# A trunk step of HGRN2, attention and convolution: four tiles instead of three grow during the first modulation, and the background modulation is paced differently

## The chip, the cores and the metric

The kernel runs on one core of a Trainium2 chip. The metric is the device time of one execution in microseconds (us), the median of several runs. PE is TensorE, DVE is VectorE, ACT is ScalarE, POOL is GpSimd and SP is SyncE, whose queue carries most loads.

## What is computed

Two trunk layers work on 640 tokens (128 of context, 512 latent) with 2048 channels. Cut to what matters here:

```python
def trunk_layer(x, shift, scale, gate, w_in_l, w_out_l, ...):
    h = x * (1 + scale) + shift
    z = h @ w_in_l
    aq, ak, av, ag, hq, hi, hff, hfb, hgate, ca, cb, cgate = jnp.split(z, SPLIT_POINTS, axis=-1)
    ...
    mix = jnp.concatenate([att * silu(ag), hg_out * silu(hgate), cv_out * silu(cgate)], axis=-1)
    out = mix @ w_out_l
    x_new = layer_norm(ALPHA * x + gate * out, ln_w_l, ln_b_l)
```

Shift, scale and gate of each layer are `silu(cond) @ ada_w_l + ada_b_l`, the modulation. The three branches are an HGRN2 gated recurrence in both directions (4 heads), windowed attention (8 heads) and a convolution over 31 positions with a layer norm.

## The kernel before

**The projections.** Tokens lie along the free dimension. The input projection of a layer is 52 tiles of 128 output channels by 640 tokens (list `NTILES`): tiles 0 to 15 are `hff, hfb, hi, hq` of the four HGRN heads, 16 to 19 the HGRN gates, 20 to 31 attention, 32 to 39 the convolution (`cb`, `ca` of four channel blocks), 40 to 51 gates. A float32 product is made of three products of rounded parts (`HH` and `HL` of the activations, `wh` and `wl` of the weights), so a tile takes 16 k-rows x 3 products x 2 pieces (256 and 384 columns, L1173 and L1175) = 96 matmuls. A tile accumulates in PSUM: `zt[0]` and `zt[1]` hold 1024 columns each, two banks (columns 0 to 511 and 512 to 1023), and `mb[0]` to `mb[3]` are one bank each. A tile in `zt` uses columns 256 to 511 and 512 to 895. Weights come in pieces of 256 KB, `raw` by SP's queue; ACT rounds them (L290, L286), and the low part comes by a second load that POOL issues (L292) or by a subtraction on DVE (L287).

**Stage 1.** The first layer's shift and scale are needed before anything else: `ada_pe` streams 64 tiles `adaw` of 512 KB through SP's queue, multiplies each on PE (four matmuls at L317), and for each of 8 steps `n` and 2 parts sums the result (two transposes at L327). After a step, two k-rows of `h` are built, and `start_mm(n - 1)` grows `NS` = 3 projection tiles by the two k-rows of the step before (12 matmuls a tile). The last block, `start_mm(7)`, runs after the last step. The fourth tile (tile 3, `hq` of head 0) is the first of the main loop.

**The main loop.** Each tile is 8 pieces of 12 matmuls, and after each piece `pump(3, rate)` lets up to three steps of the waiting generators emit their instructions: evacuations (`e_hf` takes a sigmoid and a logarithm of `hff` and `hfb` and scans them, `e_hi` copies, `e_hq` takes a Silu), the HGRN heads (`hg_main`), attention, convolution (`e_ca`, L1027 per tap) and its layer norm (`conv_ln`). The program thus fixes the order on each engine.

**HGRN.** A head works at levels 64, 32, 16, 8 and finer: POOL subtracts (L521, L524), ACT takes exponentials, DVE multiplies (L533, L534; L606, L607 at a finer level), PE multiplies in blocks of 32 (L540, in `compact`).

**Background modulation.** The other modulations, (layer, part) = (0,2), (1,1), (1,0) in layer 0 and (1,2) in layer 1, run on DVE: `ada_dve` loads 64 tiles `adawD` each and makes 256 products each at L362; a step is two products. Their pace is a credit: each pump adds `rate` to it and each whole unit buys a step.

```python
            rate = RATE[l][0 if i < 20 else 1 if i < 32 else 2 if i < 45 else 3]
```

In the output projection, which works in groups of columns, `pump(1, RWO ...)` does the same. By the program's order a main-loop tile has 4 to 10 such steps.

**The convolution's layer norm.** `total` adds four channel blocks (L1047, L1048), `split` parts the sum (L286, L287), PE sums over channels with ones (L426, L427), and L1068 subtracts the mean. ACT's squares (L1072) follow, and behind them, in ACT's order, an evacuation (L1096) and roundings of weights (L290, L291), from which POOL's L292 loads are issued.

## Time and profile before

| | |
|---|---|
| runs | 2252.66, 2254.46, 2255.24 us; median 2254.46 |
| profiled execution | 2252.99 us, its span 2251.1 us, so 1.9 us lie around the span |
| mean granted clock of PE | 0.992 |
| busy share of PE | 97% |
| HBM read | 383.46 MB |

The profile shows one execution. "Busy" is time in which the engine ran an instruction; "idle before, releaser" is time in which the engine stood and what ended it. A timeline row is the start in us, the duration, engine, line, operation, tile written and tiles read; in brackets the idle time before it and the instruction that ended it. A window row gives the busy time of every engine in a stretch.

### The profile page before, as it was taken

The numbers are of one execution on the slowest core, as the hardware profiler recorded it, in microseconds if no ns is written. First come the engines' busy times: TensorE is split into PE (matmuls) and PEld (weight loads), VectorE is DVE, ScalarE is ACT, GpSimd is POOL, SyncE is SP. The second block draws the span as 40 slices with busy tenths as digits, with TensorE's granted clock in tenths as the row PEclk, the third lists the DMA queues.
The fourth block names the chain that finished last, engine by engine and source line by source line (L and its number), as shares of the span: only waits on it lengthen the run. The fifth ranks groups of instructions, "written<-read, shape, count | busy, mean of one in ns | idle before, by whom it ended". The sixth has DMA issues, their size and how long they took to land.

```text
span 2251.1 us, 42122 instructions
## 1 busy us (share of the span) xinstructions
PE 2178.7 (97%) x15854; PEld 2077.2 (92%) x15854; DVE 1472.3 (65%) x3795; ACT 1142.6 (51%) x2047; POOL 616.0 (27%) x704
## 2 busy tenths in 40 slices
PE   6899999999999999999989999999999999999995
PEld 3699999999999999988989999999999999998895
DVE  2488889557669998676673666534655877234458
ACT  1177877546565335511165878764556543551111
POOL 0034334332222243300032344433222133330005
PEclk9999999999999999999999999999999999999998
DMA  9978787887777789964435777788776577685332
GB/s 371 400 191 203 184 200 188 206 218 182 170 159 170 190 193 229 272 197 135 118 130 135 160 173 163 158 193 186 162 153 129 114 170 157 144 196 178 96 97 103
DMA packets 210716, 403.60 MB, mean 179 GB/s; under 512 B 24816, under 2 KB 30672, under 8 KB 209872
## 3 DMA queue, kind: packets, MB, share of 16 engines
q1 hardware_dynamic: 138992, 271.85, 38.3%
q0 software_dynamic: 61600, 116.96, 30.3%
q10 hardware_dynamic: 9920, 12.10, 1.7%
q8 instruction: 124, 2.03, 0.4%
q14 instruction: 80, 0.66, 0.1%
HBM read 383.46 MB, written 12.11 MB: 176 GB/s over the span
## 4 chain that ended last, share of the span: by engine, by line
PE 77%; DVE 11%; DMA 4%; issue 3%; ACT 3%; POOL 1%; ACTq 0%; SPq 0%; DVEq 0%; POOLq 0%
PE z L1175 31%; PE z L1173 21%; PE z L1432 9%; PE m L1432 8%; DVE junk L362 4%; DMA x<-adaw 2%; PE m L948 2%; PE m L862 2%; PE m L916 1%; DMA s<-xT 1%; PE m L664 1%; DVE y1y L1414 1%; ACT s L1392 1%; DVE s L534 1%; DVE y1y L1415 0%
## 5 line engine op out<-in xcount | busy, mean ns | idle before, releaser
L1175 PE MATMUL z<-HH,wh 128*128 128x384 f32 x3296 | 1045.8, 338 | 0.0
L1173 PE MATMUL z<-HH,wh 128*128 128x256 f32 x3296 | 926.4, 283 | 1.6 <-DVE wh L287 0.9
L292 POOL DMA_DIRECT2D wh<-win x388 | 344.4, 933 | 1090.8 <-ACT wh L291 1021.5
L1173 PEld LDWEIGHTS z<-HH,wh 128*128 128x128 f32 x3296 | 619.4, 189 | 5.5 <-DVE wh L287 1.6
L1175 PEld LDWEIGHTS z<-HH,wh 128*128 128x128 f32 x3296 | 620.0, 188 | 1.5
L1175 PE MATMUL z<-HL,wh 128*128 128x384 f32 x1648 | 557.6, 338 | 0.0
L362 DVE SCALAR_TENSOR_TENSOR junk<-raw,s 128x256 bf16<-128x256 f32 x1024 | 503.8, 492 | 52.1 <-DMA raw<-adawD 24.4
L1173 PE MATMUL z<-HL,wh 128*128 128x256 f32 x1648 | 461.3, 280 | 0.0
L1173 PEld LDWEIGHTS z<-HL,wh 128*128 128x128 f32 x1648 | 311.0, 189 | 0.0
L1175 PEld LDWEIGHTS z<-HL,wh 128*128 128x128 f32 x1648 | 309.9, 188 | 0.0
L291 ACT ACTIVATE wh<-wh 128x512 fp32r<-128x512 f32 x400 | 253.1, 633 | 79.4 <-PE z L1175 68.4
L290 ACT CAST wh<-raw 128x512 fp32r<-128x512 f32 x400 | 244.0, 610 | 71.2 <-issue 36.2
L286 ACT CAST wh<-raw 128x512 fp32r<-128x512 f32 x136 | 83.0, 621 | 305.0 <-PE m L1432 156.6
L1027 DVE SCALAR_TENSOR_TENSOR s<-s,sm,s 128x655 f32<-128x655 f32 x240 | 231.2, 963 | 6.3
L1432 PE MATMUL z<-wh,HH 128*128 128x512 f32 (+1 forms) x640 | 182.0, 368 | 0.0
L1432 PE MATMUL m<-wh,HH 128*128 128x512 f32 (+1 forms) x640 | 173.8, 357 | 0.0
L287 DVE TENSOR_TENSOR wh<-raw,wh 128x512 fp32r<-128x512 f32 x138 | 92.6, 687 | 122.9 <-ACT wh L286 120.2
L1432 PEld LDWEIGHTS z<-wh,HH 128*128 128x128 f32 x640 | 116.1, 189 | 20.0
L1432 PEld LDWEIGHTS m<-wh,HH 128*128 128x128 f32 x640 | 114.1, 189 | 17.5
L1432 PE MATMUL z<-wh,HL 128*128 128x512 f32 (+1 forms) x320 | 117.7, 368 | 0.0
L1432 PE MATMUL m<-wh,HL 128*128 128x512 f32 (+1 forms) x320 | 114.3, 357 | 0.0
L1096 ACT ACTIVATE s<-z 128x640 f32<-128x640 f32 x32 | 22.5, 703 | 151.6 <-PE z L1175 142.8
(555 smaller groups left out, 2745.2 us busy)
## 6 DMA issues: line engine op xcount, KB each, us to landing
raw<-win SPq DMA_DIRECT2D x416, 256.0 KB, 4.2
wh<-win POOLq DMA_DIRECT2D x388, 256.0 KB, 5.5
raw<-adawD SPq DMA_DIRECT2D x256, 256.0 KB, 4.0
x<-adaw SPq DMA_DIRECT2D x64, 512.0 KB, 8.3
raw<-wout SPq DMA_DIRECT2D x128, 256.0 KB, 2.8
s<-crow SPq DMA_DIRECT2D x32, 256.0 KB, 5.9
s<-xT ACTq DMA_DIRECT2D x16, 320.0 KB, 7.1
s<-s ACTq DMA_DIRECT2D x80, 64.0 KB, 3.8
```

What stands on the lines that cost most here:

```text
L286: act.copy(hi, src)
L287: (lo_eng or dve).tensor_tensor(lo, src, hi.bitcast(F32), op=ALU.subtract)
L290: act.copy(hi, r)
L291: act.activation(lo, hi.bitcast(F32), AF.Copy, scale=-1.0)
L292: pool.dma_start(out=lo, in_=w.bitcast(F32R), accum_op=ALU.add)
L362: dve.scalar_tensor_tensor(junk, r[:, 256 * n:256 * n + 256], 1.0, rows[0][:, 256 * c:256 * c + 256], op0=ALU.mult, op1=ALU.mult, accum_ou ...
L862: pe.matmul(b[:, 0:w], lhsT=a_, rhs=k_, start=(n_ == 0), stop=(n_ == 2))
L948: pe.matmul(o, lhsT=v_, rhs=p_, start=(y == 0 and n_ == 0), stop=(y == len(bl) - 1 and n_ == 2))
L1027: dve.scalar_tensor_tensor(acc, u[:, t:t + AW], sm[:, cw + t:cw + t + 1], acc, op0=ALU.mult, op1=ALU.add)
L1173: pe.matmul(za, lhsT=w_, rhs=h_[:, 0:2, k, :], start=st_, stop=sp_)
L1175: pe.matmul(zb, lhsT=w_, rhs=h_[:, 2:5, k, :], start=st_, stop=sp_)
L1432: pe.matmul(bs[tt][:, 0:w], lhsT=h_[:, tt, k, :], rhs=w_[:, o:o + w], start=(k == 0 and n_ == 0), stop=(k == KT - 1 and n_ == 2))
```

## The change

`NS` becomes 4, so all four tiles of head 0 grow in stage 1. A class `Z` describes a tile by its two pieces. Tiles 0 and 1 stay in `zt[0]` and `zt[1]`. Tile 2 takes the free columns 0 to 255 of `zt[1]` and bank `mb[2]`; tile 3 those of `zt[0]` and `mb[3]`. Tile 0 and tile 3 so share bank 0 of `zt[0]`, and tiles 1 and 2 share bank 0 of `zt[1]`. Two matmuls of zeros open these banks, and the pieces in them neither start nor stop an accumulation. A `zt` is given back when both its tiles are evacuated, so the first tile of the main loop, now tile 4, takes `mb[0]` and `mb[1]`. Evacuations of the four take two instructions. The pace of layer 0's background modulation goes from (1.0, 0.85, 0.5, 1.2) to (0.6, 1.0, 0.6, 1.3), and in the output projection from 4/3 to 2.0.

```diff
--- before.py
+++ after.py
@@ -45,7 +45,7 @@
 W0 = 4
 WN = (0, 3, 4)
 CY = 5
-RWO = 4 / 3
+RWO = 2.0
 ODMA = 6
 WKEEP = 3
 FL = 3
@@ -71,7 +71,7 @@
 SMW = _o
 
 ADAD = [(0, 2), (1, 1), (1, 0), (1, 2)]
-RATE = ((1.0, 0.85, 0.5, 1.2), (0.5, 0.5, 0.0, 0.8))
+RATE = ((0.6, 1.0, 0.6, 1.3), (0.5, 0.5, 0.0, 0.8))
 BLOCK = object()
 
 
@@ -221,11 +221,22 @@
     pool.dma_start(out=crow.rearrange("a c k -> (a c) k"), in_=crs[0:16, 0:256])
     S.put(crs)
 
+    class Z:
+
+
+        def __init__(self, a, b, put, opens=True, closes=True):
+            self.a, self.b, self.put, self.opens, self.closes = a, b, put, opens, closes
+
     def zput(z):
-        if isinstance(z, tuple):
-            M.put(*z)
+        if isinstance(z, Z):
+            z.put()
         else:
             ZP.put(z)
+
+    def zparts(z):
+        if isinstance(z, Z):
+            return (slice(0, 256), z.a), (slice(256, T), z.b)
+        return ((slice(0, T), z[:, 256:896]),)
 
     def load_consts():
         sync.dma_start(out=cos, in_=A["cos"])
@@ -450,7 +461,8 @@
         st = hgset[l, j]
         Kt, GG, _, _ = hv(l, st)
         kd = Kt[:, T * d:T * d + T]
-        act.activation(kd, zsb(z), AF.Sigmoid, scale=-1.0)
+        for x, v_ in zparts(z):
+            act.activation(kd[:, x], v_, AF.Sigmoid, scale=-1.0)
         zput(z)
         yield
         s = yield from S.get()
@@ -483,11 +495,8 @@
         yield from wait(("hgset", l, j))
         v = hv(l, hgset[l, j])[3]
         s = yield from S.get()
-        if isinstance(z, tuple):
-            act.copy(s[:, 0:256], z[0][:, 256:512])
-            act.copy(s[:, 256:640], z[1][:, 0:384])
-        else:
-            act.copy(s[:, 0:T], zsb(z))
+        for x, v_ in zparts(z):
+            act.copy(s[:, x], v_)
         zput(z)
         yield
         yield
@@ -497,7 +506,8 @@
 
     def e_hq(l, j, z):
         yield from wait(("hgset", l, j))
-        act.activation(hv(l, hgset[l, j])[2], zsb(z), AF.Silu)
+        for x, v_ in zparts(z):
+            act.activation(hv(l, hgset[l, j])[2][:, x], v_, AF.Silu)
         zput(z)
         flags.add(("hq", l, j))
         yield
@@ -1160,7 +1170,8 @@
 
 
     def mm(l, i, z, ks, halves):
-        za, zb = (z[0][:, 256:512], z[1][:, 0:384]) if isinstance(z, tuple) else (z[:, 256:512], z[:, 512:896])
+        za, zb = (z.a, z.b) if isinstance(z, Z) else (z[:, 256:512], z[:, 512:896])
+        opens, closes = (z.opens, z.closes) if isinstance(z, Z) else (True, True)
         za = za.rearrange("p (a b) -> p a b", b=P)
         zb = zb.rearrange("p (a b) -> p a b", b=P)
         for k in ks:
@@ -1170,13 +1181,29 @@
             for n_, (w_, h_) in enumerate(((wh, HH), (wh, HL), (wl, HH))):
                 st_, sp_ = (k == 0 and n_ == 0), (k == KT - 1 and n_ == 2)
                 if 0 in halves:
-                    pe.matmul(za, lhsT=w_, rhs=h_[:, 0:2, k, :], start=st_, stop=sp_)
+                    pe.matmul(za, lhsT=w_, rhs=h_[:, 0:2, k, :], start=st_ and opens,
+                              stop=sp_ and closes)
                 if 1 in halves:
                     pe.matmul(zb, lhsT=w_, rhs=h_[:, 2:5, k, :], start=st_, stop=sp_)
 
 
-    NS = 3
-    zs = [zt[0], zt[1], (mb[2], mb[3])]
+    NS = 4
+    share = [2, 2]
+
+    def zs_put(n, *ms):
+        def put():
+            M.put(*ms)
+            share[n] -= 1
+            if not share[n]:
+                ZP.put(zt[n])
+        return put
+
+    zs = [Z(zt[0][:, 256:512], zt[0][:, 512:896], zs_put(0), False, False),
+          Z(zt[1][:, 256:512], zt[1][:, 512:896], zs_put(1), False, False),
+          Z(zt[1][:, 0:256], mb[2][:, 0:384], zs_put(1, mb[2]), False),
+          Z(zt[0][:, 0:256], mb[3][:, 0:384], zs_put(0, mb[3]), False)]
+    for z in zt:
+        pe.matmul(z[:, 0:512], lhsT=zd[0][:, 0:128], rhs=zd[0][:, 0:512], start=True, stop=False)
     M.f = deque(mb[0:2])
     ZP.f.clear()
     for k in range(6):
@@ -1252,8 +1279,12 @@
         for i in range(first):
             enqueue(i, zs[i] if l == 0 else zt[i])
         for i in range(first, NN):
-            pump_until(lambda: ZP.f)
-            z = ZP.f.popleft()
+            if l == 0 and i == first:
+                m0, m1 = M.f.popleft(), M.f.popleft()
+                z = Z(m0[:, 256:512], m1[:, 0:384], lambda: M.put(m0, m1))
+            else:
+                pump_until(lambda: ZP.f)
+                z = ZP.f.popleft()
             if i == HOLD0:
                 hold.add(0)
             rate = RATE[l][0 if i < 20 else 1 if i < 32 else 2 if i < 45 else 3]
```

Three places show what moves. First ACT at the end of stage 1. The names are `h00kt` (the gates of head 0), `z_99` and `z_100` (the tiles `zt[0]`, `zt[1]`), `m_` (a bank `mb`), `s_` (scratch). Before:

```order
L453 ACT_TABLE_LOAD
L453 ACTIVATE h00kt<-z_99 128x640
L461 ACT_TABLE_LOAD
L461 ACTIVATE s_143<-s_143 128x640
L453 ACT_TABLE_LOAD
L453 ACTIVATE h00kt<-z_100 128x640
L487 COPY s_137<-m_103 128x256
L488 COPY s_137<-m_104 128x384
```

And in the changed kernel:

```order
L465 ACT_TABLE_LOAD
L465 ACTIVATE h00kt<-z_99 128x256
L465 ACTIVATE h00kt<-z_99 128x384
L465 ACTIVATE h00kt<-z_100 128x256
L465 ACTIVATE h00kt<-z_100 128x384
L499 COPY s_143<-z_100 128x256
L499 COPY s_143<-m_103 128x384
L301 CAST wh_430<-raw_254 128x512
L302 ACTIVATE wh_431<-wh_430 128x512
L473 ACT_TABLE_LOAD
```

The evacuations come in two pieces, the four sigmoids stand together, and the logarithms (L461, now L473) behind the copies of tile 2. The piece of tile 0 in `z_99`'s first bank stands behind the last matmul of tile 3 in that bank; before, it stood behind tile 0's own last matmul.

Second, DVE in head 1 of layer 0 between levels 32 and 8 (`h01kt`, `h01q`: that head's gates and queries; L362 is the background's product). Before:

```order
L533 TENSOR_TENSOR s_137<-s_137,h01kt 128x2x10x32
L534 SCALAR_TENSOR_TENSOR s_1973<-s_1973,h01q 128x640
L362 SCALAR_TENSOR_TENSOR junk,aacc<-raw_250,s_135 128x256 x2
L362 SCALAR_TENSOR_TENSOR junk,aacc<-raw_516,s_135 128x256 x4
L362 SCALAR_TENSOR_TENSOR junk,aacc<-raw_518,s_135 128x256 x2
L533 TENSOR_TENSOR s_143<-s_143,h01kt 128x2x20x16
L534 SCALAR_TENSOR_TENSOR s_117<-s_117,h01q 128x640
L362 SCALAR_TENSOR_TENSOR junk,aacc<-raw_518,s_135 128x256 x2
L533 TENSOR_TENSOR s_139<-s_139,h01kt 128x2x40x8
```

And now, where L533, L534 and L362 are L543, L544 and L373:

```order
L543 TENSOR_TENSOR s_197<-s_197,h01kt 128x2x10x32
L544 SCALAR_TENSOR_TENSOR s_143<-s_143,h01q 128x640
L373 SCALAR_TENSOR_TENSOR junk,aacc<-raw_258,s_141 128x256 x4
L543 TENSOR_TENSOR s_2004<-s_2004,h01kt 128x2x20x16
L544 SCALAR_TENSOR_TENSOR s_2005<-s_2005,h01q 128x640
L373 SCALAR_TENSOR_TENSOR junk,aacc<-raw_168,s_141 128x256 x2
L543 TENSOR_TENSOR s_135<-s_135,h01kt 128x2x40x8
```

Between levels 32 and 16 stood 8 products and now 4; heads 2 and 3 have 6 there, and before every head of the layer had 8. From the level-8 product to the first one at L607 there were 8 in head 1, and now 4. In layer 1 nothing moves.

Third, DVE at the convolution's layer norm of layer 0, from the last addition of the sum (L1048, now L1058) over the split (L287, now L298) to the first subtraction of the mean (L1068, now L1078). Before:

```order
L1048 TENSOR_TENSOR s_143<-s_143,s_7282 128x640
L362 SCALAR_TENSOR_TENSOR junk,aacc<-raw_246,s_2825 128x256 x4
L362 SCALAR_TENSOR_TENSOR junk,aacc<-raw_166,s_3508 128x256 x4
L362 SCALAR_TENSOR_TENSOR junk,aacc<-raw_248,s_3508 128x256 x4
L287 TENSOR_TENSOR s_8607<-s_143,s_8606 128x640
L362 SCALAR_TENSOR_TENSOR junk,aacc<-raw_162,s_3508 128x256 x4
L362 SCALAR_TENSOR_TENSOR junk,aacc<-raw_246,s_3508 128x256 x4
L1068 SCALAR_TENSOR_TENSOR a00k<-m_102,s_6780 128x128
```

And now:

```order
L1058 TENSOR_TENSOR s_139<-s_139,s_6419 128x640
L373 SCALAR_TENSOR_TENSOR junk,aacc<-raw_164,s_145 128x256 x2
L373 SCALAR_TENSOR_TENSOR junk,aacc<-raw_168,s_145 128x256 x4
L373 SCALAR_TENSOR_TENSOR junk,aacc<-raw_260,s_2005 128x256 x4
L373 SCALAR_TENSOR_TENSOR junk,aacc<-raw_258,s_2005 128x256 x4
L298 TENSOR_TENSOR s_8523<-s_139,s_8522 128x640
L373 SCALAR_TENSOR_TENSOR junk,aacc<-raw_164,s_2005 128x256 x4
L373 SCALAR_TENSOR_TENSOR junk,aacc<-raw_168,s_2005 128x256 x4
L373 SCALAR_TENSOR_TENSOR junk,aacc<-raw_256,s_2005 128x256 x4
L373 SCALAR_TENSOR_TENSOR junk,aacc<-raw_258,s_2005 128x256 x2
L1078 SCALAR_TENSOR_TENSOR a00k<-m_104,s_5851 128x128
```

There were 12 products ahead of the split and 8 behind it, and now there are 14 and 14. Over the convolution as a whole, the background products from the first attention step after the tile `ca` 0 to the split go up by 22 (11 pairs). By the same order, from tile 20 to the split there are 48 more than before. Every group of the output projection but the last has 24 in place of 16. No product is added or removed in all.

## Rows read from the trace of the kernel before

**Rows 1.** Page, parts 1 and 5 of the whole run: busy time by engine; one costly group.

```profile
PE 2178.7 (97%) x15854; PEld 2077.2 (92%) x15854; DVE 1472.3 (65%) x3795; ACT 1142.6 (51%) x2047; POOL 616.0 (27%) x704
...
L362 DVE SCALAR_TENSOR_TENSOR junk<-raw,s 128x256 bf16<-128x256 f32 x1024 | 503.8, 492 | 52.1 <-DMA raw<-adawD 24.4
```

**Rows 2.** Waits of PE, whole run: us in total, times, longest us.

```profile
PE m L317 <- DMA x<-adaw: 19.1, 15, 6.7
PE m L327 <- DVE s L323: 11.9, 16, 3.6
```

**Rows 3.** Windows: length, then busy PE, PEld, DVE, ACT, POOL, PEclk, DMA share, GB/s.

```profile
90.60:103.30 12.70, 11.61 (x105) 9.25 (x104) 4.69 (x12) 1.46 (x2) 0.00 (x0) 0.85 1.02 408
103.30:114.30 11.00, 9.90 (x105) 7.55 (x105) 6.50 (x15) 3.02 (x5) 0.00 (x0) 1.00 1.04 400
114.30:125.00 10.70, 10.70 (x75) 10.70 (x75) 6.95 (x15) 7.47 (x10) 0.00 (x0) 1.00 0.60 200
125.00:139.60 14.60, 14.60 (x102) 14.58 (x101) 11.75 (x28) 11.28 (x18) 6.11 (x6) 1.00 0.72 174
```

**Rows 4.** Timeline of ACT and of DVE, first evacuation.

```profile
121.03 1.28 ACT L453 ACT_TABLE_LOAD   x1
122.32 0.70 ACT L453 ACTIVATE h00kt<-z 128x640 f32<-128x640 f32 x1
...
127.26 1.49 DVE L465 TENSOR_TENSOR_SCAN h00gg<-scanm,s 128x640 f32<-128x640 bf16 x1
```

**Rows 5.** Waits of PE, HGRN of layer 0 (125 to 420), then of layer 1.

```profile
PE m L540 <- DVE s L534: 5.0, 4, 1.4
PE m L540 <- DVE s L607: 3.1, 4, 1.3
...
PE m L540 <- DVE s L607: 1.1, 1, 1.1
```

**Rows 6.** Timelines of DVE and PE, head 1 of layer 0; idle before in brackets.

```profile
221.17 6.16 DVE L362 SCALAR_TENSOR_TENSOR junk<-raw,s 128x256 bf16<-128x256 f32 x1
...
228.66 0.82 DVE L533 TENSOR_TENSOR s<-s,h01kt 128x640 f32<-128x640 f32 x1
...
231.69 0.82 DVE L534 SCALAR_TENSOR_TENSOR s<-s,h01q 128x640 f32<-128x640 f32 x1
...
232.56 0.56 PE L540 MATMUL m<-s,s 128*32 128x32 f32 x40 [1.36 <-DVE s L534]
```

**Rows 7.** Timeline of POOL, the same stretch.

```profile
221.59 1.58 POOL L521 TENSOR_TENSOR s<-h01gg 128x640 f32<-128x640 f32 x1
```

**Rows 8.** Windows (columns as above), then timeline of DVE, convolution of layer 0.

```profile
640.00:660.00 20.00, 20.00 (x144) 19.87 (x144) 9.74 (x41) 13.26 (x29) 4.53 (x8) 1.00 0.72 165
...
780.00:800.00 20.00, 20.00 (x138) 20.00 (x137) 19.44 (x38) 5.65 (x10) 5.21 (x6) 1.00 0.87 201
...
757.45 0.29 DVE L1015 TENSOR_TENSOR s<-z,s 128x128 f32<-128x128 f32 x1 [1.36 <-PE z L1175]
...
758.26 0.90 DVE L1027 SCALAR_TENSOR_TENSOR s<-s,sm,s 128x655 f32<-128x655 f32 x1
...
759.88 2.77 DVE L1027 SCALAR_TENSOR_TENSOR s<-s,sm,s 128x655 f32<-128x655 f32 x3
```

**Rows 9.** Timelines of DVE and PE, convolution's layer norm, layer 0.

```profile
851.59 0.82 DVE L287 TENSOR_TENSOR s<-s,s 128x640 fp32r<-128x640 f32 x1
...
855.92 0.34 PE L427 MATMUL m<-s,ones 128*128 128x384 f32 x1
```

**Rows 10.** POOL's timeline, its line from 860 to 866, PE's timeline.

```profile
863.55 0.88 POOL L292 DMA_DIRECT2D wh<-win  x1 [1.50 <-ACT wh L291]
...
DMA to landing us min/median/max: 4.3/4.9/5.5
...
870.99 0.28 PE L1173 MATMUL z<-HH,wh 128*128 128x256 f32 x1
```

**Rows 11.** Timeline of DVE, start of layer 0's output projection.

```profile
957.03 0.42 DVE L362 SCALAR_TENSOR_TENSOR junk<-raw,s 128x256 bf16<-128x256 f32 x1 [10.04 <-DMA raw<-adawD]
```

## The prediction

> **What bounds the kernel now.** I read the page first: PE is busy for 97% of the span and DVE for 65% [rows 1]. So time can come only from PE's waits, or from where PE works at a lower clock, and the question for each edit is which wait it removes or makes. The list of PE's waits comes next. Two of them belong to stage 1: 19.1 us for the modulation's tiles and 11.9 us for DVE's sums of them [rows 2]. The windows then cut stage 1 into its steps: in 90.6 to 103.3 the DMA engines are full (share 1.02) and PE's mean granted clock is 0.85, so part of that step ran at the lower of its two levels; in 103.3 to 114.3 PE is busy for 9.90 of 11.00 us; from 114.3 on it never waits [rows 3]. In layer 0's HGRN part, PE waits eight times for DVE's multiplications, 5.0 + 3.1 = 8.1 us, and once, 1.1 us, in layer 1 [rows 5]. In the convolution PE waits for nothing, but DVE is busy for 19.44 of 20 us [rows 8]: that is where a little more work shows.
>
> The sum is made against the profiled execution, 2252.99 us (span 2251.1); the median of the runs shown is 1.5 us above it. About 0.2%, 4.5 us, is what a measurement of this kernel tells from no change.
>
> **Stage 1: gain 6.5 us.** The last two blocks of three tiles, 72 matmuls, take 10.70 us [rows 3], so a tile's 96 take 14.3 and its share of one block (12 matmuls) 1.78. Before, tile 3 ran alone in 125.0 to 139.6 [rows 3]. Now its eight blocks lie in stage 1. Two of them stand in the last two blocks, where PE never waits: 3.6. One stands in the step that PE bounds already: 1.8. The other five, 8.9 us, lie in steps in which PE waits for tiles, 19.1 us in all [rows 2]: nothing, except that 1 MB of weights more goes through the same full DMA engines. At the windows' 400 GB/s that is 2.6 us; I take 1.9, since step 90.6 to 103.3 was held partly by PE at the lower clock (bounds 1.3 and 2.6). Stage 1 thus ends 1.9 + 1.8 + 3.6 = 7.3 us later, at 132.2, with 14.3 us of tile 3 done: 7.0 gained. A fall of the clock like that in the window with 0.85 costs 0.15 x 12.7 = 1.9; I take off 0.5 for its chance. Bounds: 14.3 - 8.0 - 1.9 = 4.4, and 14.3 - 6.7 = 7.6. The two opening matmuls stand at the program's start, before the first tile has landed; if that cover were gone they would cost two matmuls of 512 columns, under 1 us by the 0.34 of one with 384 [rows 9].
>
> **The change of stages: loss 1.5 us.** ACT began on tile 0 at 121.0, inside the last block [rows 4]. Now tile 0's first piece shares a bank with tile 3, and the order shows its sigmoid behind tile 3's last matmul in that bank, so ACT begins at 132.2. Up to head 0's exponentials it then makes four table loads of 1.28 and some 16 passes of about 0.70 [rows 4], 16.3 us, to 148.5; a multiplication pair of 0.82 each, begun before the last exponential, ends by about 149.8. PE comes to head 0's products 1 1/8 tiles after the stage, at 132.2 + 16.1 = 148.3. So PE waits about 1.5 (0, if the scans and roundings overlap as they did; 3, if POOL holds DVE once as it did at 221.17 [rows 6]). The rest of the order does not move on PE: heads 1 to 3 stand where they stood. What no row of the kernel before shows is a bank shared by two tiles. The Trainium skill, PSUM — Partial Sum Buffer, section "PSUM bank collisions raise a hardware error", says that two engines may not touch one bank in the same partitions at once, at different columns either, and that the hardware does not stall but errs. That speaks against this change: it is why the wait can't be dropped. Were tile 0 evacuated as early as before, this term would be 0 and the sum 1.5 lower; no run yet shows it.
>
> **HGRN of layer 0: gain 6.8 us.** In head 1 an L362 takes 6.16 us, because POOL subtracts beside it from 221.59 on [rows 6, 7]. Three more products follow, then level 16 is multiplied from 228.66, and PE's wait for level 8 is 1.36 at 232.56 [rows 6]. With 4 products in place of 8, those that remain are over before POOL begins; level 16 can begin when POOL lets go at about 227.3, 1.3 earlier, and the wait goes or leaves 0.1. Ahead of L607 four products of 0.49 [rows 1] fewer give 2.0 against waits of 1.3 at most [rows 5]. Layer 1, with 4 products per gap, has a single wait of 1.1 [rows 5]. So of 8.1 us I take 6.8, leaving one wait as long as layer 1's or a little more; bounds 5 and 8.1. What is late next is nothing: PE's own products follow.
>
> **Attention: nothing.** Just ahead of the convolution, in 640 to 660, DVE is busy for 9.74 of 20 us [rows 8], which covers two products more a tile; with that cover gone they would be late as in the convolution.
>
> **The convolution of layer 0: loss 4.7 us.** In the stretch before the layer norm 22 products are added, 11 pairs. A pair between two taps costs 1.62 - 0.92 = 0.69 us (758.26 to 759.88, against a third of 2.77) [rows 8], so 7.6. DVE's one wait for PE there, 1.4 us, takes up some, and half of the 0.56 us in each of some five windows, another 1.4 [rows 8]: DVE is 4.8 late at the split. The split ended at 852.4 and PE needed it at 855.92 [rows 9], 3.5 later: PE waits 1.3. Behind the split stand 14 products of 0.49, so the subtraction of the mean begins at 852.4 + 4.8 + 6.9 = 864.1, in place of 856.3 (right behind PE's 855.92 + 0.34), 7.8 late. Queued behind it on ACT are squares, an evacuation and the roundings from which POOL issues loads: one was issued at 863.55, landed 4.3 later, and PE needed it at 870.99 [rows 10], 3.1 in hand. PE itself is 1.3 later, so it waits another 7.8 - 1.3 - 3.1 = 3.4. Bounds: 0, if DVE takes up all, and 4.1 + 3.4 = 7.5, if nothing.
>
> **Output projection of layer 0: nothing.** Each of three groups gets 8 products more, 3.9 us, in a stretch where DVE once waits 10.04 us for its tiles [rows 11]. Bounds 0 and 3.9.
>
> Sum: -6.5 + 1.5 - 6.8 + 4.7 = -7.1, so 2245.9 as the profiled execution counts, and **2247.4** as median. Its own range, from the likelier part of the bounds, is 2242 to 2253.
>
> **The rivals.**
>
> *DVE takes up the convolution's products.* For: the lateness is a difference of estimates. Against: 19.44 of 20. Time: -11.8, 2242.7.
>
> *Stage 1 gives nothing*, that is, the change doesn't do what it says: PE, which runs in order, is what ends each step, and the fourth tile only moves. For: 11.61 of 12.70 and 9.90 of 11.00 are busy. Against: 19.1 us of waits for tiles. Time: -6.8 + 1.5 + 4.7 = -0.6, 2253.9.
>
> *HGRN's waits stay*, because POOL and ACT set them and not the count of products. For: the multiplication can't begin before about 227.3 in any case, and every wait is short. Against: 3 products of those 8 lie behind that point. Time: -6.5 + 1.5 + 4.7 = -0.3, 2254.2. The Trainium skill, SBUF — State Buffer, section "Who interferes with whom", calls the ports that VectorE shares with GpSimd an exclusive lock. By that rule a multiplication with two inputs in SBUF is held as the product was, and this rival follows wherever POOL ends late; the trace agrees, with 6.16 for a product that takes 0.49 in the mean.
>
> *Slower: DVE never catches up from tile 20 on.* All 48 products that the order adds up to the split are late there: 48 x 0.49 = 23.5. The wait is then 23.5 - 3.5 = 20.0, and 3.4 behind it, so the sum is -11.8 + 23.4 = +11.6, 2266. It decides from a lateness of 16.4 us on (below 11.9 the change still gains). For: the convolution has no room, and its taps are one chain that waits in DVE's order. Against: from 640 to 660 DVE is idle for half the time [rows 8], which should take the attention's share, and it waits for PE once later, 1.4 us.
>
> **How the numbers follow.** The forecast 0.48, no loss in the convolution 0.20, no gain in stage 1 0.10, HGRN's waits stay 0.10, slower 0.12. The first has most of its own range (0.40) below 2249.9, which is faster by over 0.2%; with the second and a little of the next two that makes 0.62 faster, 0.24 the same and 0.14 slower. The range 2240 to 2255 holds the first two cases nearly whole and the next two by their centres; it leaves out the slower case and the ends.
>
> **What would show it.** Right: stage 1's last block ends near 132; PE's waits for L534 and L607 (now L544 and L617) fall from 8.1 to about 1; a wait of PE for the convolution's split and one for a weight piece some 15 us behind it, 4 to 5 us together. Wrong: a last block near 139 or a clock below 1.00 in it (stage 1); the L540 matmuls (now L550) waiting as before (HGRN); no wait at the split (first rival) or one above 12 us (slower).

## The result and the profile after

The changed kernel takes 2278.16 us (median of 5 runs, 2275.49 to 2281.34) against 2254.46 (5 runs of the kernel before): a ratio of 1.0105, 95% interval 1.0092 to 1.0119. It is 24 us slower, where 7 us faster was forecast. The profiled execution took 2281.34 us, the slowest of the five; its span is 2279.6, 28.5 more than before, so the parts below add up to more than the 24 us of the medians.

The first view is the busy time by engine, and the list of PE's waits (us in total, times, longest):

```profile
PE 2190.3 (96%) x15858; PEld 2084.8 (91%) x15858; DVE 1449.9 (64%) x3799; ACT 1136.8 (50%) x2045; POOL 613.8 (27%) x700
```

```profile
PE m L328 <- DMA x<-adaw: 13.1, 12, 6.9
PE m L338 <- DVE s L334: 12.5, 16, 4.2
PE m L438 <- DVE s L298: 6.8, 2, 5.0
...
PE m L550 <- DVE s L544: 5.7, 2, 4.5
PE m L583 <- DVE s L544: 3.6, 1, 3.6
PE m L872 <- DVE ats L887: 3.2, 1, 3.2
PE m L550 <- DVE s L617: 3.0, 3, 1.6
...
PE m L865 <- DVE wh L298: 2.4, 2, 2.3
PE z L1184 <- DMA wh<-win: 2.0, 3, 1.0
```

PE's busy share says almost nothing (97% before). The list does. L328 is the modulation's wait (L317 before) and fell from 19.1 to 13.1 [rows 2]: the fourth tile does fill waits of stage 1. Five waits that the kernel before did not have, or had shorter, matter below: L438 (the layer norm of the convolution), L583 and one L550 of 4.5 us (head 0), L872 and L865 (attention).

To see what each part lost, I take the start of a tile's first matmul in PE's timeline, before and after, and the growth of the difference from one to the next. The same is done for every experiment below (us, profiled executions; minus is faster than before; "end" is the span). The profiled executions lie up to 3.2 us from the medians that are given with the experiments, so a row shows where time goes and a median how much:

| run | stage 1, to tile 4 | passage and head 0, 4 to 8 | HGRN, 8 to 20 | attention, 20 to 37 | conv taps, 37 to 46 | layer norm, 46 to 50 | rest of layer 0 | layer 1, end | sum |
|---|---|---|---|---|---|---|---|---|---|
| changed kernel | -2.9 | +12.2 | -3.9 | +10.2 | 0.0 | +11.8 | -0.2 | +1.2 | +28.5 |
| e1 pace only | +0.4 | -2.1 | -6.9 | +5.8 | 0.0 | +6.5 | 0.0 | +0.3 | +3.9 |
| e2 four tiles only | -5.7 | +12.4 | +3.1 | +1.5 | 0.0 | +0.9 | +0.3 | +1.6 | +14.2 |
| e3 later pace back | -6.6 | +12.4 | -3.9 | +3.6 | 0.0 | +0.3 | +30.5 | +0.9 | +37.2 |
| e4 scan late | -7.4 | +6.0 | -3.9 | +11.1 | 0.0 | +11.9 | 0.0 | +1.6 | +19.2 |
| e5 and quiet tile 4 | -5.0 | +3.3 | -3.9 | +5.8 | 0.0 | +13.2 | +1.0 | +1.2 | +15.6 |
| e6 and mixed pace | -7.0 | +4.5 | -3.0 | -0.5 | 0.0 | +10.1 | +0.1 | +1.4 | +5.6 |
| e7 slower in HGRN | -7.2 | +3.3 | -3.8 | +2.8 | 0.0 | +3.8 | +11.5 | +2.5 | +13.0 |
| e8 three tiles, mixed | +1.1 | -2.1 | -6.8 | +0.6 | 0.0 | +6.8 | 0.0 | +0.8 | +0.5 |
| e9 four, 1.2 late | -6.6 | +4.5 | -1.0 | -0.1 | 0.0 | +7.4 | 0.0 | +0.5 | +4.7 |
| e10 three, 1.2 late | +1.4 | -2.1 | -3.5 | +3.1 | 0.0 | +0.8 | -0.2 | +0.4 | -0.1 |
| e11 changed, 1.2 late | -4.4 | +12.3 | -3.9 | +8.5 | 0.0 | +11.4 | 0.0 | +2.4 | +26.2 |
| e12 before, 1.3 late | +1.4 | -0.4 | -0.1 | +0.3 | 0.0 | +0.7 | 0.0 | +1.2 | +3.1 |
| e13 changed, one stream | -6.9 | +11.4 | -3.9 | +7.0 | 0.0 | +6.8 | -0.1 | +1.9 | +16.2 |
| e14 four, one stream | -6.4 | +4.3 | -3.0 | +2.1 | 0.0 | +1.8 | +2.0 | +1.7 | +2.5 |
| e15 three, one stream | +0.5 | -2.1 | -6.2 | -0.2 | 0.0 | -0.1 | +1.7 | +1.5 | -5.0 |

The changed kernel's loss thus has three places, each of 10 to 12 us, and no loss between them: what is late there stays there.

**Stage 1** in the windows (length, then busy PE, PEld, DVE, ACT, POOL, PE's clock, DMA share, GB/s), with two later stretches:

```profile
39.20:55.50 16.30, 13.20 (x117) 9.12 (x117) 4.70 (x12) 1.45 (x2) 0.00 (x0) 0.88 0.99 369
...
109.80:122.60 12.80, 11.70 (x119) 9.36 (x118) 7.10 (x16) 3.55 (x6) 0.00 (x0) 1.00 1.04 398
...
157.50:164.30 6.80, 5.36 (x35) 5.24 (x36) 2.16 (x5) 3.96 (x8) 0.70 (x1) 0.50 0.50 107
174.60:181.40 6.80, 5.25 (x57) 5.22 (x58) 6.58 (x16) 4.36 (x6) 0.86 (x1) 0.50 0.81 206
```

The step that PE bounded, 11.0 us before [rows 3], takes 12.8: the 1.8 of the forecast. The first step runs partly at the lower clock, 0.88. In the last two rows, which lie in head 0, PE ran at half its clock for 6.8 us each.

**The passage.** PE's timeline (idle before and its releaser in brackets):

```profile
136.75 0.28 PE L1184 MATMUL m<-HH,wh 128*128 128x256 f32 x1
...
158.94 0.80 PE L583 MATMUL m<-s,s 128*64 128x64 f32 x10 [3.63 <-DVE s L544]
...
176.15 0.76 PE L550 MATMUL m<-s,s 128*32 128x32 f32 x40 [4.52 <-DVE s L544]
```

Tile 4 begins at 136.75 (`m`: it grows in banks `mb`). Two waits follow. DVE's timeline shows what was late:

```profile
145.87 5.79 DVE L373 SCALAR_TENSOR_TENSOR junk<-raw,s 128x256 bf16<-128x256 f32 x1
...
155.07 3.81 DVE L544 SCALAR_TENSOR_TENSOR s<-s,h00q 128x640 f32<-128x640 f32 x1
...
172.24 1.49 DVE L477 TENSOR_TENSOR_SCAN h01gg<-scanm,s 128x640 f32<-128x640 bf16 x1 [2.16 <-ACT s L473]
...
174.44 0.82 DVE L543 TENSOR_TENSOR s<-s,h00kt 128x640 f32<-128x640 f32 x1
```

POOL's shows its subtractions beside them, the first of four in a row and the first of two:

```profile
146.07 1.59 POOL L531 TENSOR_TENSOR s<-h00gg 128x640 f32<-128x640 f32 x1
...
155.33 1.58 POOL L531 TENSOR_TENSOR s<-h00gg 128x640 f32<-128x640 f32 x1
```

And ACT's shows its last exponential for level 32:

```profile
151.40 0.74 ACT L538 ACTIVATE s<-s 128x640 f32<-128x640 f32 x1 [0.52 <-POOL s L534]
```

The first wait: a product is held for 5.79, then level 32's L544 itself for 3.81 in place of 0.82, both while POOL subtracts. ACT was done at 152.14, 3.2 us before PE came to this product at 155.31, so PE did not wait for ACT. The second: level 8 of head 0 (L543 at 174.44) stands in DVE's order behind the scan of head 1's first gates (`h01gg`), and that waits until 172.24 for ACT's logarithm. The waits, with 0.7 for a transpose, are 3.6 + 4.5 + 0.7 = 8.8; half of PE's busy time in the two half-clock windows, 2.7 + 2.6, is by estimate lost besides; less the two waits of before in this head, 1.35 and 0.61, that makes 12.1 of the 12.2.

**Attention.** DVE's timeline at two turns of the rotary embedding, whose halves are exchanged by DMA, in the changed kernel:

```profile
489.88 0.69 DVE L751 TENSOR_TENSOR s<-s,cos 128x512 f32<-128x512 f32 x1 [6.94 <-DMA s<-s]
...
506.15 0.69 DVE L751 TENSOR_TENSOR s<-s,cos 128x512 f32<-128x512 f32 x1 [4.47 <-DMA s<-s]
```

the second of them in the kernel before:

```profile
496.86 0.69 DVE L741 TENSOR_TENSOR s<-s,cos 128x512 f32<-128x512 f32 x1 [2.14 <-DMA s<-s]
```

and PE's timeline of the changed kernel behind them:

```profile
530.85 0.44 PE L872 MATMUL m<-a00k,a00qa 128*128 128x384 f32 x1 [3.19 <-DVE ats L887]
...
652.10 0.49 PE L865 MATMUL m<-s,a01op 128*128 128x128 f32 x2 [2.27 <-DVE wh L298]
```

PE is 5.5 us behind the kernel before in this stretch (the table's first three columns), DVE at 506.15 is 9.3 behind: 3.8 late, though it stood idle for 4.47 just before. ACT's timeline shows the transfers that DVE waits for being issued (ACTq is ACT's queue of issues):

```profile
481.29 3.95 ACTq L749 DMA_DIRECT2D s<-s  x4
...
498.69 0.62 ACT L890 ACTIVATE wh<-wh,ats 128x384 f32<-128x384 f32 x1 [1.29 <-DVE ats L887]
...
500.25 2.46 ACTq L749 DMA_DIRECT2D s<-s  x4
```

The first is issued at 481.29, as far behind the kernel before (475.78) as PE is, but DVE can use its result only 8.6 us later, where it took 6.0 before. That makes DVE 2.6 late. The second stands on ACT behind a wait for DVE, so it is issued 2.6 late. At the next turn, where DVE has no idle time before it in either kernel, it is 4.7 late, 0.9 more, which is two products of some 0.47 (their spacing in DVE's timeline). PE's wait of 3.19 comes behind this, and then DVE also stands for the first rows (`crow`) of the next background modulation:

```profile
542.91 0.43 DVE L373 SCALAR_TENSOR_TENSOR junk<-raw,s 128x256 bf16<-128x256 f32 x1 [4.74 <-DMA s<-crow]
```

**The layer norm of the convolution.** DVE:

```profile
872.71 0.82 DVE L298 TENSOR_TENSOR s<-s,s 128x640 fp32r<-128x640 f32 x1
...
893.54 2.13 DVE L384 SCALAR_TENSOR_TENSOR scl<-s,sm 128x32 f32<-128x32 f32 x1
...
899.69 0.42 DVE L373 SCALAR_TENSOR_TENSOR junk<-raw,s 128x256 bf16<-128x256 f32 x1 [4.02 <-DMA s<-crow]
...
900.51 0.82 DVE L298 TENSOR_TENSOR s<-s,s 128x640 fp32r<-128x640 f32 x1
```

PE:

```profile
873.59 0.45 PE L438 MATMUL m<-s,ones 128*128 128x384 f32 x1 [1.79 <-DVE s L298]
...
901.38 0.49 PE L438 MATMUL m<-s,ones 128*128 128x384 f32 x1 [4.99 <-DVE s L298]
...
921.02 0.39 PE L1184 MATMUL z<-HH,wh 128*128 128x256 f32 x1 [1.00 <-DMA wh<-win]
```

The first split costs a wait of 1.79, which answers to [rows 9], where PE had 3.5 in hand. The second costs 4.99, and there DVE did not work: one background modulation ended (L384), the next had not loaded its rows (`crow`), and DVE stood for 4.02 with the second split behind it in its order. Behind the wait at each split PE ran at half its clock:

```profile
874.30:877.70 3.40, 3.40 (x15) 3.40 (x14) 3.13 (x17) 0.00 (x0) 0.26 (x1) 0.50 1.03 211
901.60:905.00 3.40, 3.40 (x15) 3.40 (x15) 3.12 (x17) 3.06 (x5) 0.00 (x0) 0.51 0.65 204
```

The four waits of PE in this stretch (the fourth is 0.77 at 891.3, for a weight piece) make 8.6 us, 7.9 more than the 0.67 before; with half of the two windows, 3.4, that is 11.3 of the 11.8.

### The profile page after: what moved, and what is told of

It is laid out like the page before. It is cut to its first block, busy times and chain, and to the rows that moved or that the text cites. A ratio compares the mean times of both kernels' runs of the same rounds, so it can differ in the third digit from the quotient of the medians.

```text
span 2279.6 us, 42132 instructions
## 1 busy us (share of the span) xinstructions
PE 2190.3 (96%) x15858; PEld 2084.8 (91%) x15858; DVE 1449.9 (64%) x3799; ACT 1136.8 (50%) x2045; POOL 613.8 (27%) x700
## 4 chain that ended last, share of the span: by engine, by line
PE 52%; DVE 13%; issue 5%; ACT 3%; POOL 2%; DMA 1%; ACTq 0%; POOLq 0%; DVEq 0%
PE z L1187 18%; PE z L1184 12%; PE z L1463 9%; PE m L1463 8%; DVE s L1037 5%; DVE junk L373 3%; PE m L958 1%; PE m L872 1%; PE m L926 1%; POOL s L534 1%; DMA wh<-win 1%; ACT wh L301 1%; POOL s L531 1%; ACT s L1423 1%; DVE y1y L1445 1%
## 5 line engine op out<-in xcount | busy, mean ns | idle before, releaser
L1187 PE MATMUL z<-HH,wh 128*128 128x384 f32 x3232 | 1029.6, 340 | 0.0
L1187 PE MATMUL z<-HL,wh 128*128 128x384 f32 x1616 | 548.9, 340 | 0.0
L373 DVE SCALAR_TENSOR_TENSOR junk<-raw,s 128x256 bf16<-128x256 f32 x1024 | 472.9, 462 | 50.7 <-DMA raw<-adawD 16.8
L298 DVE TENSOR_TENSOR wh<-raw,wh 128x512 fp32r<-128x512 f32 x142 | 94.9, 687 | 108.2 <-ACT wh L297 108.1
```

What stands on the lines that cost most here:

```text
L298: (lo_eng or dve).tensor_tensor(lo, src, hi.bitcast(F32), op=ALU.subtract)
L373: dve.scalar_tensor_tensor(junk, r[:, 256 * n:256 * n + 256], 1.0, rows[0][:, 256 * c:256 * c + 256], op0=ALU.mult, op1=ALU.mult, accum_ou ...
L1187: pe.matmul(zb, lhsT=w_, rhs=h_[:, 2:5, k, :], start=st_, stop=sp_)
```

## The experiments

**First set: the two halves of the change, the later pace, and the scan.**

e1, the pace alone, in the kernel before:

```diff
-RWO = 4 / 3
+RWO = 2.0
-RATE = ((1.0, 0.85, 0.5, 1.2), (0.5, 0.5, 0.0, 0.8))
+RATE = ((0.6, 1.0, 0.6, 1.3), (0.5, 0.5, 0.0, 0.8))
```

> The kernel before with the new pace alone (three tiles in stage 1). Theory A, the loss lies in three separate places and adds up: the attention and convolution parts lose as in the changed kernel (about 10 and 12 us there), HGRN gains about 6 by its waits: +14 to +18, about 2270. Rival B, the four tiles' later start runs on through the later parts, and the pace itself is harmless: -6, about 2248.

Measured 2257.52, ratio 1.0014 (1.0005 to 1.0023). By the table HGRN gains 9.0 in all (its waits are gone: no wait of PE is left between 125 and 420 us), attention loses 5.8 and the layer norm 6.5. The losses come without four tiles, so rival B falls; they are half as large as expected, so the sum, +3.7, is far below the +14 to +18.

e2, four tiles alone: the changed kernel with both lines above turned back.

> The changed kernel with the old pace and the old rate of the output projection (four tiles in stage 1). Theory A: stage 1 gives 3 us, the passage into head 0 loses 12 to 18 (more background products stand between head 0's multiplications), heads 1 to 3 wait as in the kernel before, attention and convolution lose nothing: +9 to +15, about 2264 to 2270. Rival B: the late start alone makes the attention and convolution waits, so as slow as the changed kernel, 2278.

Measured 2269.14, ratio 1.0068 (1.0051 to 1.0085). Attention and layer norm lose 1.5 and 0.9, so they are the pace's; the passage loses 12.4 with either pace. The two halves add up: 3.7 + 15.3 = 19 of the 24 us, the rest lies in attention and layer norm, which lose more when both are there.

e3, the old pace from tile 20 on:

```diff
-RWO = 2.0
+RWO = 3.3
-RATE = ((0.6, 1.0, 0.6, 1.3), (0.5, 0.5, 0.0, 0.8))
+RATE = ((0.6, 0.85, 0.5, 1.2), (0.5, 0.5, 0.0, 0.8))
```

> The changed kernel with the old pace from tile 20 on (0.85, 0.5, 1.2), the first part at the new 0.6, and 3.3 in the output projection, which takes the 30 steps that are left. Theory A: the waits of attention (10 us with what the clock loses) and of the convolution (12) go, the output projection has room or loses up to 5: 2257 to 2262. Rival B: 2278. A second rival, that the output projection cannot take the steps: waits of PE there or at its end, above 2265.

Measured 2289.18, ratio 1.0155 (1.0140 to 1.0170): the slowest of all, by the second rival. Attention and layer norm go down to 3.6 and 0.3, as theory A has it, but the output projection loses 30.5. It now has up to 40 steps, 80 products, in each of three groups, and PE waits there for DVE's multiplications by the gate, which read the finished banks:

```profile
1015.58 0.80 PE L1463 MATMUL m<-wh,HH 128*128 128x512 f32 x1 [10.32 <-DVE s L1367]
```

So a step that is taken away at one place has to be paid where it goes; 48 products a group cost nothing or, in three later runs, 1.0 to 2.0, 80 cost 30 us, and 60 (e7, below) 11.5.

e4, the scan of head 1's first gates emitted six steps later:

```diff
         act.activation(u, u, AF.Ln, bias=1.0, scale=-1.0)
         yield
+        if (l, j, d) == (0, 1, 0):
+            for _ in range(XY):
+                yield
```

with `XY = 6`, which puts it behind level 8 and two finer levels of head 0.

> The changed kernel with head 1's first scan emitted six steps later, behind head 0's level 8 on DVE. Theory A, the scan, which waits for ACT's logarithm, holds head 0's level-8 multiplication: the 4.5 us wait of PE shrinks by 3 to 4 and the fall of the clock behind it goes or stays: -3 to -7.5, 2271 to 2275. Rival C, level 8 is late by ACT's and POOL's chain in any case: within 1 us of the changed kernel, 2278.

Measured 2271.59, ratio 1.0075 (1.0060 to 1.0090): 6.6 better than the changed kernel, and the passage falls from +12.2 to +6.0. PE's second wait:

```profile
167.31 0.56 PE L554 MATMUL m<-s,s 128*32 128x32 f32 x40 [1.11 <-DVE s L548]
```

1.11 in place of 4.52, and no fall of the clock behind it. The scan is shown as the cause of about half of the passage's loss.

**Second set: the other half of the passage, and mixed paces.**

e5 is e4 with no background products while tile 4 grows:

```diff
-            rate = RATE[l][0 if i < 20 else 1 if i < 32 else 2 if i < 45 else 3]
+            rate = RATE[l][0 if i < 20 else 1 if i < 32 else 2 if i < 45 else 3] if (l, i) != (0, 4) else 0.0
```

> The run with the late scan, and besides no background products while tile 4 grows, so that none stands ahead of head 0's multiplications of levels 64 and 32. Theory A, those products push level 32 into POOL's subtractions for level 16 and so make PE's first wait of 3.6 us: it goes, with a fall of the clock that costs 2 to 3: -4 to -7 against the run with the late scan, 2265 to 2268. Rival C, ACT's chain of table loads and exponentials is the bound there: within 1.5 us of it, 2270 to 2273.

Measured 2268.64, ratio 1.0061 (1.0046 to 1.0076), 3.0 under e4; the forecast was 4 to 7. PE's timeline:

```profile
153.15 0.80 PE L587 MATMUL m<-s,s 128*64 128x64 f32 x20
...
166.25 0.56 PE L554 MATMUL m<-s,s 128*32 128x32 f32 x40 [2.81 <-DVE s L548]
```

The wait for level 32 is gone (L583 in the changed kernel), as theory A has it. But the wait for level 8 grows from 1.11 to 2.81: in ACT's timeline the two exponentials of level 8 run at 162.65 and 164.00, behind two table loads (tile 4's sigmoid comes between) and two waits for POOL, so rival C holds for the second wait. The passage is at +3.3.

e6, e7 and e8 change the pace, in e5 or in the kernel before:

```diff
 e6, from e5
+RATE = ((0.8, 0.85, 0.5, 1.3), (0.5, 0.5, 0.0, 0.8))
 e7, from e5
+RWO = 2.5
+RATE = ((0.65, 0.85, 0.5, 1.3), (0.5, 0.5, 0.0, 0.8))
 e8, from the kernel before
+RWO = 2.0
+RATE = ((0.75, 0.85, 0.5, 1.3), (0.5, 0.5, 0.0, 0.8))
```

> The same as the run with the quiet tile 4, with the pace 0.8 in HGRN, the old 0.85 and 0.5 in attention and convolution, 1.3 behind them, and 2.0 in the output projection. Theory A, the parts add up: stage 1 -6, the passage 0 to +2, HGRN -3 to -6, attention +1 to +4, convolution +1 to +2: 2244 to 2252, faster than the kernel before. Rival D, four tiles make attention late whatever the pace: 2258 or more.

Measured 2260.36, ratio 1.0031 (1.0021 to 1.0041). The time is in rival D's range, but attention is at -0.5, so rival D falls: four tiles do not make it late. The parts add up until tile 46, 5.9 ahead of before; then the layer norm loses 10.1, at the old pace of the taps. That was not expected, and it says that the taps' pace is not all that loses there.

> The same with 0.65 in HGRN and 2.5 in the output projection. Theory A: HGRN 1 to 2 us better than with 0.8, the output projection with 60 products a group somewhere between the changed kernel's 48 (no loss) and the 80 that lost 29 us: 2243 to 2256.

Measured 2267.36, ratio 1.0058 (1.0043 to 1.0073). This is above the 2243 to 2256 expected: HGRN and passage are only 0.8 and 1.2 better than in e6, and the output projection loses 11.5.

> The kernel before (three tiles in stage 1) with the pace 0.75 in HGRN, old in attention and convolution, 1.3 behind them, 2.0 in the output projection. Theory A: HGRN's waits shrink as in the run with the pace alone (there -8.7), and attention and convolution, at their old pace, lose 0 to 3: 2244 to 2250. Rival E, the attention's loss comes from where the modulations end and not from the products in a tile: it loses 5 to 6 there as with the pace alone, 2250 to 2255.

Measured 2253.35, ratio 0.9996 (0.9987 to 1.0005). The time is in rival E's range, but attention loses 0.6, so rival E falls; the layer norm loses 6.8, most of it in one wait of 4.9 at the second split.

**Third set: what loses in the layer norm.** e6 and e8 have 1.3 from tile 45 on in common, and in e8 DVE stood 3.2 us for the rows of the next modulation. e9 and e10 put 1.2 back and fit the rest; e11 does so in the changed kernel; e12 puts 1.3 into the kernel before:

```diff
 e9, from e5
+RWO = 2.1
+RATE = ((0.85, 0.85, 0.5, 1.2), (0.5, 0.5, 0.0, 0.8))
 e10, from the kernel before
+RWO = 2.0
+RATE = ((0.8, 0.85, 0.5, 1.2), (0.5, 0.5, 0.0, 0.8))
 e11, from the changed kernel
+RWO = 2.1
+RATE = ((0.6, 1.0, 0.6, 1.2), (0.5, 0.5, 0.0, 0.8))
 e12, from the kernel before
+RATE = ((1.0, 0.85, 0.5, 1.3), (0.5, 0.5, 0.0, 0.8))
```

> Four tiles, the late scan, the quiet tile 4, the pace (0.85, 0.85, 0.5, 1.2) and 2.1 in the output projection: as the run with the mixed pace, but the old 1.2 from tile 45 on. The run with the mixed pace was 5.9 us ahead of the kernel before at tile 46 and lost 10 in the convolution's layer norm. Theory F, it lost them by 12 to 16 products around the split and a weight piece behind them; here 12 and 12 stand there, as in the runs with 1.2, which lost 1 to 2: about 2249 to 2252. Rival G, the layer norm loses 7 or more whenever the parts ahead leave more steps: 2255 or more.

Measured 2259.08, ratio 1.0024 (1.0015 to 1.0034): rival G's number, the layer norm loses 7.4.

> The kernel before (three tiles) with the pace 0.8 in HGRN and 2.0 in the output projection, all else old: the run with three tiles and the mixed pace without its 1.3. That run was 7.1 ahead at tile 46 and lost 7 at the second split, where DVE waited 3.2 for the first rows of the next modulation. Theory F, here the modulation changes ahead of the second sum and not between it and its split, so that loss goes or falls below 3: 2246 to 2250. Rival G: 2253 or more.

Measured 2251.86, ratio 0.9994 (0.9985 to 1.0003). The layer norm loses 0.8, as theory F has it; the gain ahead of it was smaller than in e8 (HGRN -3.5, attention +3.1), so the time is between the two.

> The changed kernel with 1.2 in place of 1.3 from tile 45 on (2.1 in the output projection). It moves the change of modulation, a reduction and a wait for the next rows, from ahead of the second split to behind it. Theory F, that change is what makes PE's 5.0 us wait at the second split, with 1.7 of clock behind it: -5 to -8, 2270 to 2273. Rival G, the count of products is: 4 fewer, so -1 to -2, 2276 to 2277.

Measured 2276.44, ratio 1.0103 (1.0089 to 1.0116): rival G's number again. But the place has changed. DVE of e11:

```profile
897.85 0.43 DVE L373 SCALAR_TENSOR_TENSOR junk<-raw,s 128x256 bf16<-128x256 f32 x1 [5.16 <-DMA s<-crow]
```

and PE:

```profile
914.72 0.58 PE L1184 MATMUL z<-HH,wh 128*128 128x256 f32 x1 [5.61 <-DMA wh<-win]
```

The change of modulation now stands behind the second split, for which PE waits 0.68 in place of 4.99; instead what follows on DVE is 5.16 late, and PE waits 5.61 for a weight piece behind it. e9 shows the same pair, 6.26 and 5.83.

> The kernel before with 1.3 in place of 1.2 from tile 45 on and nothing else. The change of modulation stays ahead of the first sum, 12 and 6 products stand around the split. Theory F: within 2 us of the kernel before, 2252 to 2256. Rival G, the higher pace from tile 45 on is what loses: +5 to +10, 2259 to 2264.

Measured 2255.14, ratio 1.0005 (0.9996 to 1.0014): the layer norm loses 0.7, so the pace from tile 45 on does nothing by itself, and rival G falls here. In DVE's timelines, the wait for the next rows falls into this stretch in seven runs (the changed kernel, e4, e5, e6, e8, e9, e11), with 3.0 to 6.3 us, and these lose 6.8 to 13.2. The change of modulation alone does not lose: in e10 it stands between the two splits without a wait, and the layer norm loses 0.8. Nor is the wait for rows the whole loss. e1 has the change at the same place as e10, also without a wait, and loses 6.5, by PE's waits for the first split and for a weight piece:

```profile
855.52 0.45 PE L427 MATMUL m<-s,ones 128*128 128x384 f32 x1 [2.35 <-DVE s L287]
...
897.10 0.39 PE L1173 MATMUL z<-HH,wh 128*128 128x256 f32 x1 [1.81 <-DMA wh<-win]
```

And in e6 the first of two waits ends before DVE comes to the change of modulation at 878.67:

```profile
869.57 0.55 PE L1188 MATMUL z<-HH,wh 128*128 128x256 f32 x1 [4.35 <-DMA wh<-win]
```

**Fourth set: the wait at the change of modulation taken away.** e13 is the changed kernel with the three modulations of layer 0 as one stream, so that the next one's tiles and rows are loaded in time:

```diff
-    def ada_dve(l, part):
+    def ada_dve(*jobs):
-        tiles = [(kb, q) for kb in range(8) for q in range(8)]
+        tiles = [(l, part, kb, q) for l, part in jobs for kb in range(8) for q in range(8)]
...
-            if nrow <= kb or (nrow <= min(kb + 1, 7) and q == 4):
+            g = n0 // 8
+            if nrow <= g or (nrow <= min(g + 1, 8 * len(jobs) - 1) and q == 4):
...
-            adaq.extend([ada_dve(0, 2), ada_dve(1, 1), ada_dve(1, 0)])
+            adaq.append(ada_dve((0, 2), (1, 1), (1, 0)))
```

> The changed kernel with the three background modulations of layer 0 as one stream: the next one's tiles and rows are loaded while the last products of the one before run, so nothing is waited for where they change. Products 14 ahead of the first split, 8 behind it, 12 ahead of the second. Theory F, DVE's 4 to 6 us wait for rows at the change of modulation is what PE waits for in the convolution's layer norm: of the 11.7 us lost there 6 to 9 go, 2268 to 2272. Rival H, the products alone are late and the wait only stands where they would: 2275 or more.

Measured 2272.02, ratio 1.0084 (1.0070 to 1.0098), 6.1 under the changed kernel. The layer norm falls from 11.8 to 6.8, by 5.0 where theory F had 6 to 9. DVE's second split and the change of modulation behind it:

```profile
885.70 0.82 DVE L298 TENSOR_TENSOR s<-s,s 128x640 fp32r<-128x640 f32 x1
...
888.96 0.19 DVE L389 SCALAR_TENSOR_TENSOR scl<-s,sm 128x32 f32<-128x32 f32 x1
```

and PE's matmul for that split:

```profile
886.57 0.44 PE L443 MATMUL m<-s,ones 128*128 128x384 f32 x1 [0.44 <-DVE s L298]
```

0.44 in place of 4.99. The order around it moved too (8 products behind the first split and not 14), so not every part of the 5.0 us is the rows' alone; the wait for rows is gone, and with it most of the second split's wait. What is left, 6.8, is the wait of 1.79 at the first split, as in the changed kernel, one of 2.69 for weights, and a stretch of 3.4 us at half the clock behind it. No rows are waited for there, and it is as much as e1 lost, so this part is rival H's: the products' own.

e14 and e15 put the changes that helped together, with four tiles and with three: e14 is e6 with 1.2, 2.1 and one stream, e15 is e8 with 1.2 and one stream.

> Four tiles, late scan, quiet tile 4, pace (0.8, 0.85, 0.5, 1.2), 2.1 in the output projection, and the modulations as one stream. Theory F: 6 ahead of the kernel before at tile 46 as with the mixed pace, and a loss of 1 to 3 in the layer norm (18 and 12 products): 2249 to 2252. Rival H: the 7 to 10 us loss of the mixed pace stays, 2256 or more.

Measured 2255.46, ratio 1.0011 (1.0002 to 1.0020). The layer norm loses 1.8 where e6 lost 10.1; e6's wait of 4.35, which came ahead of the change of modulation, is 0.31 here, so not all of this is the stream's, and what moved that wait is open. The passage's 4.3, attention's 2.1 and 3.7 behind the layer norm leave the run behind the kernel before and above the 2249 to 2252 expected.

> Three tiles, pace (0.75, 0.85, 0.5, 1.2), 2.0 in the output projection, and one stream. Theory F: 7 ahead at tile 46 as in the run with three tiles and the mixed pace, of which the layer norm takes 0 to 2: 2246 to 2249, faster than the kernel before. Rival H: it takes 6 to 7, 2252 to 2254.

Measured 2247.56, ratio 0.9972 (0.9962 to 0.9982): faster than both kernels, by 6.2 and 30.6 us. All PE waits between 125 and 420 us in it:

```profile
PE z L1178 <- DMA wh<-win: 0.4, 1, 0.4
```

It is the pace that gains, in HGRN, when nothing else pays for it; the fourth tile is not in it. Of the 6.8 that e8 lost in the layer norm nothing is left, but e15 has the stream and the 1.2 at once; e10, with 1.2 and without the stream, lost 0.8, so the stream's own part was not measured with three tiles.

## Why the prediction was wrong

The two gains that were forecast are there, HGRN's in the changed kernel only in part; three losses that were put at nothing, 1.5 and 4.7 are 10 to 12 each.

**Stage 1: right.** Forecast -6.5, bounds 4.4 and 7.6. Eleven profiles with four tiles gave -2.9 to -7.4, eight of them -5.7 or better, -6.6 in the middle (against one profile of the kernel before; five others with three tiles came to tile 4 up to 1.4 later). The changed kernel's own profile is the worst, outside the bounds; its first two steps ran partly at the lower clock (0.88 in the first window above). What else made the spread is open: e5, whose clock did not fall before tile 4, gained 5.0. The two opening matmuls, priced at under 1 us, took 3.78 (as four records):

```profile
2.50 3.78 PE L1206 MATMUL z<-zd 128*128 128x512 f32 x4 [2.50 <-POOL zd L211]
```

They were over at 6.28, and PE then waited for the first tile until 6.46 (6.72 in the kernel before), so the cover held. The rival that nothing is gained falls.

**The change of stages: wrong, +12.2 with head 0 against 1.5 less head 0's share of HGRN's gain.** The step that failed is "the rest of the order does not move on PE". It is true of PE, but DVE was not looked at behind level 32: there the scan of the next head, which waits for ACT, had moved ahead of head 0's level 8 (e4, with the scan later, loses 6.2 less of the 12.2). The wait for level 32 was forecast at 1.5, as the lateness of ACT's chain, at most 3 if POOL held DVE once. ACT took 11.7 us to head 0's exponentials (136.78 to 148.51) and not 16.3, and was not what PE waited for. POOL held DVE twice, a product for 5.79 and L544 for 3.81, and the wait was 3.63; products at that place decide it (e5). The Trainium skill, SBUF — State Buffer, section "Who interferes with whom", says that a VectorE instruction with two inputs in SBUF contends with a GpSimd instruction that reads there; the trace agrees, and here for the multiplication itself (3.81 in place of 0.82) and not only for products. The other rule weighed, the Trainium skill's PSUM — Partial Sum Buffer, section "PSUM bank collisions raise a hardware error", could only be seen in the order: ACT's timeline has the table loaded at 129.27 and the first sigmoid

```profile
136.78 0.38 ACT L465 ACTIVATE h00kt<-z 128x256 f32<-128x256 f32 x1 [6.22 <-PE z L1184]
```

behind the last matmul in the shared bank. What a read beside it would do wasn't tried. The estimate of this term had nothing for the clock, which by estimate took 5.3 of the 12.2.

**HGRN: the mechanism right, the size not.** Forecast -6.8 in all four heads, bounds 5 and 8.1. With the pace alone (e1) it is 9.0 (2.1 in head 0), more than the waits that were counted; where the rest comes from is open. In the changed kernel heads 1 to 3 gain 3.9, since two waits of 1.2 stay, and head 0 gains nothing. The rival that the waits stay because POOL and ACT set them falls, except for head 0 with four tiles.

**Attention: wrong, +10.2 against 0.** The step that failed is that DVE's idle half from 640 to 660 covers two products more a tile. That window is emptier than the seven before it. From 500 to 640 in the kernel before, DVE is busy for 13.0 to 15.7 us of each 20, and at the four turns of the rotary embedding from 517 to 592 it has no idle time in front. One such window:

```profile
520.00:540.00 20.00, 19.69 (x142) 19.45 (x140) 14.69 (x58) 11.40 (x28) 5.33 (x6) 1.00 0.80 189
```

In e1, with the same pace, DVE is 0.2 and 0.4 late at the third and fourth turn, where it had 5.4 and 2.5 us of idle time, and then 1.3, 2.0 and 3.3 late at the next three, where it had none: idle time did cover, and where there was none the products added up, past PE's margin. In the changed kernel the lateness starts earlier, with a transfer that came 2.6 us later than before, and idle time does not cover this, since it ends with a DMA that ACT issues behind work which waits for DVE. Why that transfer took longer is open; one of 9.0 us stands at the same place in e14, at the pace 0.85. The pace of 1.0 lost 5.8 to 11.1 in six runs, 0.85 between -0.5 and 3.6 in ten, and turning it back with the rest of the later pace took attention from 10.2 to 3.6 (e3), so the loss is mostly the pace's; the way it takes is read from traces and not tested by itself. Why 1.0 loses 5.8 in some runs and 11.1 in others stays open in the main. A part can be the 4.74 us in which DVE stands for rows at 542.91: with one stream (e13) no rows are waited for, and attention loses 7.0.

**The convolution: the mechanism right, another beside it missed.** Forecast 1.3 at the split and 3.4 at a weight piece: measured 1.79 and, in two pieces, 0.77 and 1.00. Where DVE waits for no rows (e1, e13), this mechanism with its fall of the clock loses 6.5 and 6.8, above the 4.7 and inside the bound of 7.5. The step that failed is the sum of this term, which ended with these two waits: the 4.99 at the second split, and the two falls of the clock, were not in it. In the kernel before, a background modulation ended at 798.4, among the taps; in the changed one it ends at 893.5 to 895.7, right ahead of the second split. No term was set for such a change, at which DVE waits for the loads that only then are issued.

**Output projection: right, by a wrong count.** The 24 and 16 in the text are steps of two products, so 48 and 32 products; it costs nothing all the same, and 60 would have cost 11.5.

**The slower rival** named a DVE that never catches up, 2266. The sign was right, and so was lateness in attention; but PE lost nothing more in the taps, its first loss came in the passage, and about half of the loss in the layer norm was another. Its chance was set at 0.12, against it the idle half of one window, which is the step that failed above.

## What to carry to other kernels

Before an engine's idle time is used as cover, look at every stretch and not at one window, and follow what ends it: if that comes, through other engines, from the same engine's earlier work, it need not cover lateness that is already there. When work is spread in the background at a pace, look at where its seams fall (the start, the end, the change to the next piece), since the first loads of a piece are waited for with everything queued behind; start them a piece ahead. When a change moves a start earlier on one engine, compare the order on the others for what now stands between it and its use: one scan that waits for another engine cost 6 us here, as much as the fourth tile gained.
